# Opening a transformer block with a pair of column blocks: the convolution's first gate and value product made together, in a fixed order

## The chip, the cores and the metric

The kernel runs on one core of one Trainium2 chip. The metric is the device time of the whole program in microseconds, the median over several runs. TensorE (PE) does matrix products, VectorE (DVE) and ScalarE (ACT) elementwise work, GpSimd (POOL) very little here; SyncE (SP) issues nearly all DMAs. Each engine takes its instructions in one order that is fixed when the program is built; semaphores make an instruction wait for another engine or a DMA.

## The reference

One block on 256 positions of width 4096, batch 1, all in float32. Only the beginning matters for this case:

```
xn   = rms_norm(x, norm_in_g)
proj = xn @ w_in                       # 4096 x 14336 columns
q, k, v, z_a, a_c, g_c, z_c = split(proj, 7 parts of 2048 columns)
y_a  = rms_norm(chunked_attention(q, k, v), ...) * silu(z_a)      # 16 heads of 128
u    = a_c * sigmoid(g_c)              # then a causal depthwise convolution of 31 taps
u    = silu(layer_norm(conv(u) + b_dw)); y_c = rms_norm(u @ w_pw + b_pw, ...) * silu(z_c)
h    = x + concat(y_a, y_c) @ w_out
h    = h + sigmoid(rms_norm(h) @ w_ple_gate + b) * (p @ w_ple);  out = rms_norm(h, final_g)
```

## The kernel before

**Three products for one.** Every float32 operand is split into a high part in the matmul's format `fp32r` and the remainder, also in `fp32r`: for weights `wh` (ScalarE, `parts_of`, L197) and `wl` (VectorE, L198), for activations the two halves of a `big_t` tile. A product of a 128-row block of weights with 128 positions is three matmuls of 512 columns: high by high, low by high, high by low.

**Operands from x.** `x` comes in eight pieces of 512 columns (`xin`). Each piece is turned by eight transposes of 128x128 (L156, four to a PSUM tile `tmp_ps`) and split: ScalarE writes the high half with the norm's weight (L142), VectorE the low half (L143). The two blocks of one PSUM tile go one after the other: the second block's L142 waits for the first block's L143. Each piece gives four of the 32 row blocks (k-blocks) in the list `xT`. The division by the root mean square, `r_x`, comes at the end of each product, so sums of squares (L485, ScalarE, two per piece) are all that is needed of x's norm.

**Seven products for eight.** `mixed_product` makes two column blocks of 512 at a time, for two halves of 128 positions, over 16 pairs of k-blocks. A plain pair takes 8 products (24 matmuls, L361). A pair with a star in the order list takes seven (21 matmuls) by sums of weights (`ua`, `ub`, L414 to L419, VectorE, each split as well) and sums of activations (`xS`, `combine_again`: one addition L278, four of 128x128 L260 to L263, one split L266 and L267). The seven-product pairs also write four helper banks of PSUM. Weight tiles `wt` have 5 buffers, `wh` and `wl` 3 each.

**The opening.** `gate_0 = product(...)` makes the first gate block alone: one column block, 32 k-blocks by 6 matmuls (L211). Meanwhile `load_x` brings the eight pieces of `x`, and `combine_again` makes `xS` of the first four. Its first two k-blocks use weights loaded at once by ScalarE's DMA queue (`w_first`), the order of these first steps is fixed (`pin`), the rest is left to the scheduler. Ahead of all that, five matmuls on zeros (`WARM`, L114) keep TensorE at work. Then `glu_conv(0)` makes the first value block `acca`, again 192 matmuls by `product` (L211), and multiplies it with the gate's sigmoid.

**What follows.** For each of four groups: `glu_conv(c)` (a pair of column blocks of a and g), then `heads(g)`: q and k as one pair of column blocks, v by `product`. The convolution's 31 taps by 4 blocks are 124 VectorE instructions per group (L586, L590); they wait in a list `later`, and each step of a product moves a few of them into the program (`fill`): 4 per pair of k-blocks in the paired products and 2 per step in v. The scheduler then decides where in VectorE's queue they stand. The order of pairs in these stages is

```
early = units("1 3 5 7 0* 9 2* 11 4* 13 6* 15 8 10 12 14")
```

Of the kernel before, what the change touches and what calls it, by code (L numbers as in the profile page):

```python
# [16 lines left out]
P = 128  # L17
NB = 512
KC = 2
FIRST = 2  # L20
WARM = 5
# [5 lines left out]
def hybrid_block(  # L27
# [70 lines left out]
    w_first = []  # L98
    for k in range(FIRST):
        t = wpool.tile([P, KC, NB], F32, tag="w", name="wt")  # L100
        nc.scalar.dma_start(t[:, 0, :], w_in0[k * P : (k + 1) * P, o_g : o_g + NB])
        w_first.append(t)
# [10 lines left out]
    for _ in range(WARM):  # L113
        pin(nc.tensor.matmul(idle_ps, idle[:, :P], idle, start=True, stop=True))  # L114
# [15 lines left out]
    nc.tensor.transpose(gin_ps[:, :KD], gin_rows, ident[:KD, :KD])  # L130
# [34 lines left out]
    def transposed_split(src, dst, g, col0, **kw):  # L165

        for pair in range(2):
            blocks = (2 * pair, 2 * pair + 1)
            for b, pt in zip(blocks, transposed(src, blocks, **kw)):
                split_from_psum(dst, b, pt, g[:, col0 + b : col0 + b + 1])  # L170

# [32 lines left out]
    def accumulate(acc, h, lhs, kb, wh, wl, k, kblocks, kinds=range(3), then=lambda ins: None):  # L204
# [3 lines left out]
        for kind in kinds:  # L208
            a, b = ((xh, wh), (xl, wh), (xh, wl))[kind]
            then(  # L210
                nc.tensor.matmul(  # L211
                    acc, a, b[:, k, :],
                    start=kb == 0 and kind == 0, stop=kb == kblocks - 1 and kind == 2,
                )
            )

    def product(w, col, lhs, kblocks, pool=None, tag="acc", ahead=None, given=(), fills=2):
# [4 lines left out]
        starts = list(range(len(given))) + list(range(len(given), kblocks, KC))  # L222
        for k0 in starts:
            kc = 1 if k0 < len(given) else min(KC, kblocks - k0)
            if k0 < len(given):
                wh, wl = given[k0]
                for kind in range(3):
                    for h in range(NH):
                        accumulate(acc[h], h, lhs, k0, wh, wl, 0, kblocks, (kind,))
                continue  # L230
            wh, wl = weight_parts(w, col, k0, kc)
            for k in range(kc):
                for h in range(NH):
                    accumulate(acc[h], h, lhs, k0 + k, wh, wl, k, kblocks)
                if ahead and given and k0 + k == len(given):
                    ahead(k0)
            if ahead:
                ahead(k0 + kc)
            fill(fills)
# [14 lines left out]
    def combined_parts(dst, at, s, a, a01, a11, g):  # L254
# [5 lines left out]
        nc.vector.tensor_tensor(s3, a00, a10, ALU.subtract)  # L260
        stt(s5, a11, g, a10, ALU.mult, ALU.subtract)
        stt(s2, s5, -1.0, a00, ALU.mult, ALU.subtract)
        stt(s4, a01, g, s2, ALU.mult, ALU.add)  # L263
        hi, lo = dst[:, at : at + 2, 0, :], dst[:, at : at + 2, 1, :]
        src = s.rearrange("q (i t) -> q i t", t=T)
        nc.scalar.copy(hi, src)  # L266
        nc.vector.tensor_tensor(lo, src, hi.bitcast(F32), ALU.subtract)  # L267

    def combine(dst, at, pts, g):
# [3 lines left out]
        combined_parts(dst, at, s, a[:, :T], pts[1][:, :P], pts[1][:, P:], g[:, 1:2])  # L273

    def combine_again(dst, at, t, i, rows):

        a, s = rows
        nc.vector.tensor_tensor(  # L278
            a.rearrange("q (i t) -> q i t", t=T), t[:, i : i + 2, 0, :].bitcast(F32),
            t[:, i : i + 2, 1, :].bitcast(F32), ALU.add,  # L280
        )
        combined_parts(dst, at, s, a[:, :T], a[:, T : T + P], a[:, T + P :], 1.0)
# [34 lines left out]
    early = units("1 3 5 7 0* 9 2* 11 4* 13 6* 15 8 10 12 14")  # L317
# [3 lines left out]
    def mixed_product(  # L321
        w, col, lhs, comb, order, on_helpers, ahead=None, fills=0, on_begin=None, apart=NB,
        left=(),
    ):

# [31 lines left out]
        def add(name, x, w2, n, final):  # L357

            for kind, (a, b) in enumerate(((x[0], w2[0]), (x[1], w2[0]), (x[0], w2[1]))):
# [6 lines left out]
                begun.add(name)  # L366

# [3 lines left out]

        last_seven = max(n for n, (_, seven) in enumerate(order) if seven)
        for n, (pair, seven) in enumerate(order):
            if ahead:
                ahead(pair)
            wts = []
            for k in range(2):
                wt = wpool.tile([P, 2, NB], F32, tag="w", name="wt")
                kb = 2 * pair + k
                rows = w[kb * P : (kb + 1) * P, :]  # L380
                nc.sync.dma_start(
                    wt,
                    bass.AP(
                        tensor=rows.tensor, offset=rows.offset + col,
                        ap=[list(rows.ap[0]), [apart, 2], [1, NB]],
                    ),
                )
                wts.append(wt)
            if n >= len(order) - n_left:
# [3 lines left out]
                fill(fills)  # L393
                continue
            if not seven:
                for k in range(2):
                    wh, wl = parts_of(wts[k], 2)[0]
                    for j in range(2):
                        for h in range(NH):
                            name = (("P2", "P3"), ("P4", "X"))[h][j]  # L400
                            add(name, block(2 * pair + k, h), (wh[:, j], wl[:, j]), n, k == 1)
                fill(fills)
# [42 lines left out]
            fill(fills)  # L445
# [19 lines left out]
    def scaled_pair(w, col, apart, order, r, fills):  # L465

        t, z = sum_tiles()

        def on_helpers(helper):
            nc.scalar.activation(z[0][0], helper["P1"], AF.Identity, scale=r[:, :1])  # L470
# [4 lines left out]
        c = mixed_product(w, col, xT, xS, order, on_helpers, fills=fills, apart=apart)  # L475
# [21 lines left out]
    squares = [[partial(square_sum, ssq_x[:, h, :1], x_first[:, h, :]) for h in range(NH)]]  # L497

    def load_x(c):
        xin = act.tile([P, NH, NB], F32, tag="act", name="xin")  # L500
        loaded = nc.sync.dma_start(
            xin, x[0, :, c * NB : (c + 1) * NB].rearrange("(h q) n -> q h n", q=P)
        )
        xT.append(big_tile())
        if c == 1:
            pin(loaded)
            transposed_split(xin, xT[-1], g_in, 4 * c, then=pin)
        else:
            transposed_split(xin, xT[-1], g_in, 4 * c)
        squares.append(  # L510
            [partial(square_sum, ssq_x[:, h, c : c + 1], xin[:, h, :]) for h in range(NH)]
        )
        while len(squares) > (0 if c == D // NB - 1 else 2):
            later.extend(squares.pop(0))

    def first_operands():

        given = []
        xT.append(big_tile())
        for blocks in ((0,), (1,), (2, 3)):  # L520
            for b, pt in zip(blocks, transposed(x_first, blocks)):
                made = split_from_psum(xT[0], b, pt, g_in[:, b : b + 1])
                for ins in made:
                    pin(ins)
            if len(given) < FIRST:
                parts, made = parts_of(w_first[len(given)], 1)
                for ins in made:
                    pin(ins)
                given.append(parts)
        return given, made  # L530

# [19 lines left out]
    def load_ahead(kb):  # L551

        if kb == KD // 2:
            load_parameters()
        if kb % 4 == 2 and kb // 4 + 1 < D // NB:
            load_x(kb // 4 + 1)

    given, made = first_operands()
    with tc.issue_after(made[0].ins), tc.issue_after(made[1].ins):
        gate_0 = product(w_in0, o_g, xT, KD, ahead=load_ahead, given=given)  # L560
    fill(len(later))
    r_x = rstd_of(ssq_x, D, "r_x")

    prm_ps = tmp_psum()
    nc.tensor.transpose(prm_ps[:, :n_rows], prm_rows, ident[:n_rows, :n_rows])
    prm = cpool.tile([P, n_rows], F32, name="prm")
    nc.vector.tensor_copy(prm, prm_ps[:, :n_rows])
# [3 lines left out]
    dps = tmp_psum()  # L571
    for j in range(DWC):
        nc.tensor.transpose(
            dps[:, j * DWR : (j + 1) * DWR], dw_rows[:, j, :], ident[:DWR, :DWR]
        )
    nc.vector.tensor_copy(
        dw.rearrange("q (b j) t -> q j t b", j=DWC),
        dps[:, : DWC * DWR].rearrange("q (j t b) -> q j t b", j=DWC, t=TAPS),
    )
# [15 lines left out]
    def glu_conv(c):  # L595
        if c == 0:
            sg = spool.tile([P, NH, NB], F32, tag="stage", name="sg")
            for h in range(NH):
# [544 lines left out]
```

## Time and profile before

| | |
|---|---|
| median of 3 runs | 2048.15 us (2047.39 to 2050.24) |
| the profiled execution's own time | 2047.85 us |
| its span, first to last instruction | 2046.1 us |
| TensorE busy | 2026.5 us (99%), 9131 matmuls |
| VectorE busy | 1852.8 us (91%) |
| ScalarE busy | 1167.5 us (57%) |
| first gate block, x loaded | 0 to 59.8 us |
| first value block | 59.8 to 103.9 us |
| glu_conv(1), heads(0): q and k, v | 103.9 to 190.2, to 277, to 320 us |

The profiled execution is 0.3 us under the median, and 1.75 us of it lie outside the span. In a row of the timeline stand start, duration, engine, line, operation, output and inputs, shape and count, and in brackets the idle time before it with what ended that. A row of a group has count, busy time and mean duration in ns, then the idle time just ahead. [...]

### The profile page before, as it was taken

What the parts mean: (1) busy time and instruction counts of PE and PEld (TensorE: products, weight loads), DVE (VectorE), ACT (ScalarE), POOL (GpSimd) and SP (SyncE); (2) the same over time, 40 slices, a digit from 0 to 9 for tenths busy, and PEclk for the clock granted to TensorE, in tenths of its full rate; (3) what the DMA queues carried; (4) which work ended last, traced back from release to release, by engine and by line L of the source; (5) the groups of instructions that cost most, each with busy time, mean ns of one, the idle gap of its engine ahead of it and who ended that gap; (6) DMA issues with size and microseconds to landing.
All of it is one profiled execution on the core that took longest, in us unless ns stands there. A gap on an engine that the chain in (4) does not pass through costs nothing.

```text
span 2046.1 us, 25964 instructions
## 1 busy us (share of the span) xinstructions
PE 2026.5 (99%) x9131; PEld 1667.0 (81%) x9131; DVE 1852.8 (91%) x2629; ACT 1167.5 (57%) x1503; POOL 9.8 (0%) x19
## 2 busy tenths in 40 slices
PE   9999999999999999999999999999999999999997
PEld 7888888887888788888888888888888888888876
DVE  7599999899887998865889999999999999999998
ACT  7445535554455536575556656676565666655555
POOL 0000000000000000000000000000000000000000
PEclk9999999999999999999999999999999999999999
DMA  8666665665656656555666566676656656566765
GB/s 284 186 193 208 190 193 174 196 196 190 186 188 196 198 185 189 180 186 197 193 209 200 194 216 200 217 236 206 214 199 208 210 188 207 202 220 205 236 207 179
DMA packets 166236, 412.28 MB, mean 201 GB/s; under 512 B 13006, under 2 KB 16222, under 8 KB 166106
## 3 DMA queue, kind: packets, MB, share of 16 engines
q1 hardware_dynamic: 165818, 410.11, 61.5%
q8 instruction: 71, 1.16, 0.2%
q10 hardware_dynamic: 288, 0.52, 0.1%
q14 instruction: 59, 0.48, 0.1%
HBM read 406.39 MB, written 4.19 MB: 201 GB/s over the span
## 4 chain that ended last, share of the span: by engine, by line
PE 89%; DVE 8%; issue 2%; DMA 1%; ACT 1%; SPq 0%; POOLq 0%; POOL 0%; ACTq 0%; DVEq 0%
PE acc L361 54%; PE acc L211 18%; PE acc_P L361 14%; DVE wl L198 3%; DVE cv L590 2%; PE tmp_ps L156 1%; DMA wt<-in_w_in_dram 1%; DVE ul L198 1%; PE tmp_ps L754 0%; PE tmp_ps L772 0%; DVE z L477 0%; PE tmp_ps L739 0%; ACT wh L197 0%; PE acc L350 0%; DVE ub L418 0%
## 5 line engine op out<-in xcount | busy, mean ns | idle before, releaser
L197 ACT CAST wh<-wt 128x1024 fp32r<-128x1024 f32 (+1 forms) x740 | 722.7, 985 | 616.8 <-PE acc L361 337.7
L361 PE MATMUL acc<-wh,big_t 128*128 128x512 f32 x3438 | 1064.0, 391 | 0.1
L198 DVE TENSOR_TENSOR wl<-wt,wh 128x1024 fp32r<-128x1024 f32 (+1 forms) x740 | 835.2, 1139 | 113.3 <-ACT wh L197 108.6
L361 PEld LDWEIGHTS acc<-wh,big_t 128*128 128x128 f32 x3438 | 643.7, 188 | 132.9 <-DVE z L869 0.6
L361 PE MATMUL acc<-wl,big_t 128*128 128x512 f32 x1719 | 664.5, 391 | 1.1 <-DVE wl L198 1.1
L361 PEld LDWEIGHTS acc<-wl,big_t 128*128 128x128 f32 x1719 | 322.1, 188 | 71.1 <-DVE wl L198 4.3
L211 PE MATMUL acc<-wh,big_t 128*128 128x512 f32 x1072 | 334.6, 393 | 1.0 <-DVE big_t L143 0.8
L211 PEld LDWEIGHTS acc<-wh,big_t 128*128 128x128 f32 x1072 | 201.1, 189 | 42.5 <-DVE big_t L143 1.1
L211 PE MATMUL acc<-wl,big_t 128*128 128x512 f32 x536 | 209.0, 391 | 0.0
L590 DVE SCALAR_TENSOR_TENSOR cv<-uT,dw,cv 128x237 f32<-128x237 f32 (+26 forms) x480 | 203.8, 467 | 0.9
L197 ACT CAST uh<-ub 128x1024 fp32r<-128x1024 f32 x112 | 117.8, 1052 | 116.2 <-DVE ub L419 101.7
L361 PE MATMUL acc_P<-uh,big_t 128*128 128x512 f32 x570 | 174.5, 391 | 0.0
L197 ACT CAST uh<-ua 128x1024 fp32r<-128x1024 f32 x112 | 118.0, 1054 | 58.6 <-DVE ua L415 52.3
L198 DVE TENSOR_TENSOR ul<-ub,uh 128x1024 fp32r<-128x1024 f32 x112 | 136.8, 1222 | 9.1 <-ACT uh L197 8.0
L198 DVE TENSOR_TENSOR ul<-ua,uh 128x1024 fp32r<-128x1024 f32 x112 | 136.7, 1221 | 0.5
L361 PEld LDWEIGHTS acc_P<-uh,big_t 128*128 128x128 f32 x570 | 105.9, 188 | 24.6 <-ACT uh L197 3.4
L211 PEld LDWEIGHTS acc<-wl,big_t 128*128 128x128 f32 x536 | 101.0, 188 | 20.9
L361 PE MATMUL acc_P<-ul,big_t 128*128 128x512 f32 x285 | 109.4, 392 | 1.5 <-DVE ul L198 1.5
L414 DVE TENSOR_TENSOR ua<-wt 128x512 f32<-128x512 f32 x112 | 77.0, 688 | 21.7 <-DMA wt<-in_w_in_dram 17.5
L415 DVE TENSOR_TENSOR ua<-wt 128x512 f32<-128x512 f32 x112 | 76.9, 686 | 3.1 <-DMA wt<-in_w_in_dram 3.1
L419 DVE TENSOR_TENSOR ub<-ub,wt 128x512 f32<-128x512 f32 x112 | 77.0, 688 | 1.0
L418 DVE TENSOR_TENSOR ub<-ua,wt 128x512 f32<-128x512 f32 x112 | 76.9, 687 | 0.2
(215 smaller groups left out, 1368.1 us busy)
## 6 DMA issues: line engine op xcount, KB each, us to landing
wt<-in_w_in_dram SPq DMA_DIRECT2D x447, 512.0 KB, 3.8
wt<-in_w_out_dram SPq DMA_DIRECT2D x128, 512.0 KB, 4.3
wt<-in_w_ple_gate_dram SPq DMA_DIRECT2D x128, 512.0 KB, 4.0
wt<-in_w_pw_dram SPq DMA_DIRECT2D x32, 512.0 KB, 3.9
hc<-in_x_dram SPq DMA_DIRECT2D x8, 512.0 KB, 5.5
wt<-in_w_ple_dram SPq DMA_DIRECT2D x8, 512.0 KB, 4.4
xin<-in_x_dram SPq DMA_DIRECT2D x7, 512.0 KB, 8.2
out_dram<-hc SPq DMA_DIRECT2D x12, 256.0 KB, 2.7
```

The lines of the kernel that those rows point to most:

```text
L156: nc.tensor.transpose(pt[:, i * T + h * P : i * T + (h + 1) * P], src[:, h, b * P : (b + 1) * P], ident,)
L197: nc.scalar.copy(wh[:, :kc, :], wt[:, :kc, :]),
L198: nc.vector.tensor_tensor(wl[:, :kc, :], wt[:, :kc, :], wh[:, :kc, :].bitcast(F32), ALU.subtract),
L211: nc.tensor.matmul(acc, a, b[:, k, :], start=kb == 0 and kind == 0, stop=kb == kblocks - 1 and kind == 2,)
L361: nc.tensor.matmul(banks[name], a, b, start=name not in begun, stop=final and ends[name] == n and kind == 2 and not (left and name in "P2 ...
L414: plus(ua[:, 0], w0[:, 0], w0[:, 1])
L415: plus(ua[:, 1], w0[:, 1], w1[:, 1])
L418: plus(ub[:, 0], ua[:, 0], w1[:, 1])
L419: plus(ub[:, 1], ub[:, 0], w1[:, 0])
L590: nc.vector.scalar_tensor_tensor(cv[:, i, PAD - k :], uT[:, i, : T + k - PAD], dw[:, b, k : k + 1], cv[:, i, PAD - k :], ALU.mult, ALU.add,)
```

## The change

The first gate block and the first value block become one `mixed_product` with the order list `first`: 16 pairs, of which 8, 10 and 12 take seven products. Its first nine pairs are written out by hand in `first_pairs`, every instruction pinned. Pair n needs k-blocks 2n and 2n+1, while piece n of x is loaded, transposed and split, so x is complete after eight pairs. `xS` is made of the last four pieces (`xT[4]` to `xT[7]`), between pairs 5 and 8, and `early` becomes a list whose seven-product pairs are 8, 10, 12 and 14. The parameters' transposes and copies (`parameters`, L565 to L576 before) move into this stage. `WARM` is (5, 3, 2): five matmuls on zeros as before, three behind the transpose of the norm's weights, two behind the first transposes of x. The high parts of the first two k-blocks' weights are made by VectorE (`high`). The fills are 0 in the first stage, 3 and 4 in turn in glu_conv(1) to (3), 3 in q and k, and 4 in v. Cut to its core:

```diff
-FIRST = 2
-WARM = 5
+WARM = (5, 3, 2)
...
+    w_first = [wpool.tile([P, 2, NB], F32, tag="w", name="wt") for _ in range(2)]
+    for j, col in enumerate((o_a, o_g)):
+        nc.scalar.dma_start(w_first[0][:, j], w_in0[:P, col : col + NB])
+    nc.scalar.dma_start(w_first[1], two_columns(w_in0, 1, o_a, o_g - o_a))
...
+    warm(WARM[0])
...
+    pin(nc.tensor.transpose(gin_ps[:, :KD], gin_rows, ident[:KD, :KD]))
+    warm(WARM[1])
...
-    early = units("1 3 5 7 0* 9 2* 11 4* 13 6* 15 8 10 12 14")
+    first = units("0 1 2 3 4 5 6 7 9 8* 11 10* 13 12* 15 14")
+    early = units("9 11 13 15 8* 1 10* 3 12* 5 14* 7 0 2 4 6")
...
+    def first_pairs(add):
+        def load(n): ...          # weights of pair first[n], and piece n of x
+        def parts(n, k): ...      # wh (ScalarE), wl (VectorE) of k-block k of pair n
+        def high(k, cols=slice(0, 2)):
+            pin(nc.vector.tensor_copy(made[0, k][0][:, cols], w_first[k][:, cols]))
+        def low(k): ...           # wl of the first pair
+        def operands(c, *blocks): # transposes of one PSUM tile, then L142/L143 block by block
+            pts = transposed(xin[c], blocks, then=pin)
+            for b, pt in zip(blocks, pts):
+                both = split_from_psum(xT[c], b, pt, g_in[:, 4 * c + b : 4 * c + b + 1])
+                last[:] = [*(pin(i) for i in both), *last_transpose]
+        def products(n, k, *kinds): ...
+        load(1)
+        for k in range(2):
+            made[0, k] = part_tiles()
+        for j in range(2):
+            high(0, slice(j, j + 1))
+        operands(0, 0)
+        low(0)
+        warm(WARM[2])
+        products(0, 0, (0,))
+        high(1)
+        operands(0, 1)
+        low(1)
+        products(0, 0, (1,), (2,))
+        operands(0, 2, 3)
+        for k in range(2):
+            parts(1, k)
+        products(0, 1, (0,), (1,), (2,))
+        for n in range(1, n_x + 1):
+            split = None
+            if n < n_x:
+                load(n + 1)
+                parts(n + 1, 0)
+            if n == 4:
+                load_parameters()
+            for h in range(NH):
+                pin(square_sum(ssq_x[:, h, n - 1 : n], xin[n - 1][:, h, :]))
+            if n > n_x // 2:
+                c = n - 1
+                comb = spool.tile([P, 2, NB], F32, tag="stage", name="comb")
+                split = combine_again(
+                    xS[c // 2], 2 * (c % 2), xT[c], 0, (comb[:, 0], comb[:, 1]), pin
+                )
+            products(n, 0)
+            if n < n_x:
+                xT.append(big_tile())
+                for blocks in ((0, 1), (2, 3)):
+                    operands(n, *blocks)
+                parts(n + 1, 1)
+            if split:
+                split()
+            products(n, 1)
+        parameters()
+        nc.vector.tensor_reduce(r_x, ssq_x, AX.X, ALU.add)
+        rsqrt(r_x, r_x, D)
...
-            acca = product(w_in0, o_a, xT, KD)
+            sg, gate = scaled_pair(
+                w_in0, o_a, o_g - o_a, first, r_x, (0,), begin=first_pairs
+            )
...
-            sg, gate = scaled_pair(w_in0, o_a + c * NB, o_g - o_a, early, r_x, 4)
+            sg, gate = scaled_pair(w_in0, o_a + c * NB, o_g - o_a, early, r_x, (3, 4))
...
-        q, k = scaled_pair(w_in0, o_q + g * NB, o_k - o_q, early, r_x, 4)
+        q, k = scaled_pair(w_in0, o_q + g * NB, o_k - o_q, early, r_x, (3,))
...
-        accv = product(w_in0, o_v + g * NB, xT, KD)
+        accv = product(w_in0, o_v + g * NB, xT, KD, fills=4)
```

More of the change, by code (lines that the diff above doesn't have):

```diff
@@ L112, in hybrid_block, with warm @@
     idle_ps = tmp_psum()
-    for _ in range(WARM):
-        pin(nc.tensor.matmul(idle_ps, idle[:, :P], idle, start=True, stop=True))
+    def warm(n):
+        for _ in range(n):
+            pin(nc.tensor.matmul(idle_ps, idle[:, :P], idle, start=True, stop=True))
+    warm(WARM[0])
     ident = cpool.tile([P, P], F32, name="ident")
@@ L215, in accumulate, with product @@
             )
-    def product(w, col, lhs, kblocks, pool=None, tag="acc", ahead=None, given=(), fills=2):
+    def product(w, col, lhs, kblocks, pool=None, tag="acc", fills=2):
         acc = [
@@ L221, in product @@
         ]
[L222 to L230, printed above, removed]
+        for k0 in range(0, kblocks, KC):
+            kc = min(KC, kblocks - k0)
             wh, wl = weight_parts(w, col, k0, kc)
@@ L321, in mixed_product @@
     def mixed_product(
-        w, col, lhs, comb, order, on_helpers, ahead=None, fills=0, on_begin=None, apart=NB,
-        left=(),
+        w, col, lhs, comb, order, on_helpers, ahead=None, fills=(0,), on_begin=None, apart=NB,
+        left=(), begin=None,
     ):
@@ L370, in block, with add_plain @@
             return [t[:, kb % 4, q, h * P : (h + 1) * P] for q in range(2)]
+        def add_plain(n, k, wh, wl, **kw):
+            pair = order[n][0]
+            for j in range(2):
+                for h in range(NH):
+                    name = (("P2", "P3"), ("P4", "X"))[h][j]
+                    add(name, block(2 * pair + k, h), (wh[:, j], wl[:, j]), n, k == 1, **kw)
+        done, after = 0, ExitStack()
+        if begin:
+            done, behind = begin(add_plain)
+            for ins in behind:
+                after.enter_context(tc.issue_after(ins.ins))
         last_seven = max(n for n, (_, seven) in enumerate(order) if seven)
         for n, (pair, seven) in enumerate(order):
+            if n < done:
+                continue
             if ahead:
@@ L396, in mixed_product @@
                 for k in range(2):
[L397 to L402, printed above, removed]
+                    add_plain(n, k, *parts_of(wts[k], 2)[0])
+                fill(fills[n % len(fills)])
                 continue
@@ L516, in first_operands @@
[L516 to L530, printed above, removed]
+    xS = [None] * 2 + [big_tile(upool) for _ in range(2)]
@@ L549, in load_parameters, with parameters @@
             nc.sync.dma_start(dw_rows[lo:hi], taps[lo:hi])
[L551 to L565, printed above, removed]
     prm = cpool.tile([P, n_rows], F32, name="prm")
-    nc.vector.tensor_copy(prm, prm_ps[:, :n_rows])
     ln_g, ln_b, bdw, ga, gc, gp = (prm[:, a : a + n] for a, (_, n) in zip(at, rows))
     dw = spool.tile([P, KCW, TAPS], F32, name="dw", bufs=1)
[L571 to L574, printed above, removed]
-        )
[L576 to L579, printed above, removed]
+    def parameters():
+        prm_ps = tmp_psum()
+        nc.tensor.transpose(prm_ps[:, :n_rows], prm_rows, ident[:n_rows, :n_rows])
+        nc.vector.tensor_copy(prm, prm_ps[:, :n_rows])
+        dps = tmp_psum()
+        for j in range(DWC):
+            nc.tensor.transpose(
+                dps[:, j * DWR : (j + 1) * DWR], dw_rows[:, j, :], ident[:DWR, :DWR]
+            )
+        nc.vector.tensor_copy(
+            dw.rearrange("q (b j) t -> q j t b", j=DWC),
+            dps[:, : DWC * DWR].rearrange("q (j t b) -> q j t b", j=DWC, t=TAPS),
+        )
     conv = []
@@ L813, in hybrid_block @@
     assert n_g == CW // NB
-    xS = [big_tile(upool) for _ in range(2)]
-    for c in range(4):
-        rows = spool.tile([P, 2, NB], F32, tag="stage", name="comb")
-        combine_again(xS[c // 2], 2 * (c % 2), xT[c], 0, (rows[:, 0], rows[:, 1]))
     glu_conv(0)
@@ L864, in on_helpers @@
             helper_sums(helper, z)
-        acc = mixed_product(w_in0, col + c0 * NB, xT, xS, order, on_helpers, ahead=ahead, fills=2)
+        acc = mixed_product(w_in0, col + c0 * NB, xT, xS, order, on_helpers, ahead=ahead, fills=(2,))
         for h, j in QUARTERS:
@@ L973, in gated_pair @@
         acc = mixed_product(
[L974 removed]
+            w_ple_gate[0], c0 * NB, hT, hS, order, on_helpers, ahead=ahead, fills=(4,),
             on_begin=on_begin,
```

153 lines of the change are left out of this document (77 added, 76 removed).

## The prediction

> **What bounds the kernel now.** I read the page's busy shares first, then the waits of TensorE by stretch, then the timeline of the first 25 us.
>
> ```profile
> PE 2026.5 (99%) x9131; PEld 1667.0 (81%) x9131; DVE 1852.8 (91%) x2629; ACT 1167.5 (57%) x1503; POOL 9.8 (0%) x19
> ```
> ```profile
> 22.34:59.80 37.46, 37.46 (x186) 31.31 (x185) 31.82 (x60) 29.05 (x59) 0.71 (x1) 1.00 0.73 241
> 59.80:103.90 44.10, 44.10 (x198) 36.57 (x197) 21.34 (x19) 18.92 (x19) 0.00 (x0) 1.00 0.63 191
> 103.90:190.20 86.30, 85.85 (x382) 70.43 (x381) 85.88 (x139) 43.42 (x48) 0.00 (x0) 1.00 0.63 195
> 190.20:277.00 86.80, 86.47 (x391) 71.42 (x389) 86.24 (x137) 45.42 (x50) 0.30 (x1) 1.00 0.63 201
> ```
>
> The columns of the second fence are the stretch, its length, then busy time of PE, PEld, DVE, ACT and POOL, clock, DMA share and GB/s. TensorE is the bound everywhere: the stage that makes the first value block (59.8 to 103.9 us) has it busy throughout with VectorE at half load, the paired stages behind it have both full. So time can only come from fewer matmuls, or from gaps between them, and can be lost wherever VectorE is late. The price of a matmul:
>
> ```profile
> 22.34 0.39 PE L211 MATMUL acc<-wl,big_t 128*128 128x512 f32 x1
> 22.57 0.61 PE L211 MATMUL acc<-wh,big_t 128*128 128x512 f32 x2
> 23.02 0.39 PE L211 MATMUL acc<-wl,big_t 128*128 128x512 f32 x1
> ```
>
> From 22.34 to 23.02 three have started: 0.68 / 3 = 0.227 us each. The gaps that TensorE has in the stages that the change touches:
>
> ```profile
> PE acc L361 <- DVE wl L198: 1.1, 2, 0.6
> PE tmp_ps L739 <- DVE z L477: 0.9, 3, 0.3
> PE acc_P L361 <- DVE ul L198: 0.6, 2, 0.5
> ```
>
> These are its waits between 103.9 and 730 us (total, times, longest), all for VectorE: 2.6 us to win there. The opening has more:
>
> ```profile
> 1.18 2.31 PE L114 MATMUL tmp_ps<-idle 128*128 128x512 bf16 x5 [1.18 <-DVE ssq_f L951]
> 3.42 0.31 PE L130 MATMUL tmp_ps<-ident,gin_rows 32*128 32x32 f32 x1
> 4.62 2.48 PE L156 MATMUL tmp_ps<-ident,xin 128*128 128x128 f32 x8 [0.88 <-DMA xin<-in_x_dram]
> 6.75 2.05 PE L211 MATMUL acc<-wh,big_t 128*128 128x512 f32 x4
> 9.45 0.82 PE L211 MATMUL acc<-wh,big_t 128*128 128x512 f32 x2
> 11.02 1.07 PE L211 MATMUL acc<-wh,big_t 128*128 128x512 f32 x4
> 15.00 0.50 PE L211 MATMUL acc<-wh,big_t 128*128 128x512 f32 x1 [0.20 <-ACT big_t L142]
> 16.29 0.50 PE L211 MATMUL acc<-wh,big_t 128*128 128x512 f32 x1 [0.79 <-DVE big_t L143]
> ```
>
> Four matmuls take 2.05 us at 6.75 and 1.07 at 11.02: until about 9.9 us TensorE runs at half speed (0.43 us a matmul), although the clock column reads 1.00. Full speed comes 5.3 us after its last long pause (0.88 us, ending at 4.62).
>
> **Fewer matmuls.** Before, 2 x 192 matmuls; after, 16 x 24 - 3 x 3 = 375. Nine less: 9 x 0.227 = **-2.0 us**, on the path everywhere. The five more on zeros lie in pauses.
>
> **The start.** Now TensorE works nearly without pause from 1.18: five on zeros, the transpose at 3.42, three on zeros to about 5.0, two transposes of x, two on zeros, first product at about 6.4 (6.75 before). If full speed again needs 5.3 us of work without a long pause, it comes at 6.5 instead of 9.9. Walking the fixed order with the durations below, pair 0 then runs from 6.4 to 12.5; pair 1 waits 0.4 us for `wh` and 0.75 us for `wl`, since ScalarE and VectorE do x's blocks 2 and 3 first; its last matmul, the 48th with 16 transposes behind it, starts at 19.8. Before, that count is reached at 22.34, but with 24 transposes, eight more at 0.87 us in all, so at 21.5 like for like: **-1.65 us**. If full speed comes at 9.9 all the same, the walk gives -0.45; without pair 1's waits -2.8. I take -1.65, as nothing but the pause distinguishes the two starts.
>
> [...]
>
> **The fixed order of pairs 1 to 8.** This is the largest term. Two blocks of one PSUM tile follow in lockstep:
>
> ```profile
> 7.13 0.47 ACT L142 ACTIVATE big_t<-tmp_ps,g_in 128x256 fp32r<-128x256 f32 x1
> 7.96 0.48 DVE L143 SCALAR_TENSOR_TENSOR big_t<-tmp_ps,g_in,big_t 128x256 fp32r<-128x256 f32 x1
> 8.47 0.48 ACT L142 ACTIVATE big_t<-tmp_ps,g_in 128x256 fp32r<-128x256 f32 x1 [0.87 <-DVE big_t L143]
> 8.98 0.49 DVE L143 SCALAR_TENSOR_TENSOR big_t<-tmp_ps,g_in,big_t 128x256 fp32r<-128x256 f32 x1 [0.54 <-ACT big_t L142]
> ```
>
> The second L143 starts 1.02 us after the first, 0.54 of it idle. The scheduler of before put two tiles side by side (or `wl` between); the hand order does tile by tile, so VectorE waits 0.54 us twice a piece. The other durations of this stretch:
>
> ```profile
> L198 DVE TENSOR_TENSOR wl<-wt,wh 128x1024 fp32r<-128x1024 f32 x29 | 35.5, 1225 | 26.6 <-ACT wh L197 26.2 <-PE tmp_ps L156 0.4
> L143 DVE SCALAR_TENSOR_TENSOR big_t<-tmp_ps,g_in,big_t 128x256 fp32r<-128x256 f32 x24 | 10.6, 479 | 0.3 <-ACT big_t L142 0.3
> L278 DVE TENSOR_TENSOR comb<-big_t 128x512 f32<-128x512 f32 x4 | 2.7, 687 | 0.1
> L267 DVE TENSOR_TENSOR big_t<-comb,big_t 128x512 fp32r<-128x512 f32 x4 | 2.7, 686 | 0.7 <-ACT big_t L266 0.7
> L576 DVE COPY dw<-tmp_ps 128x496 f32<-128x496 f32 x1 | 1.1, 1085 | 0.2 <-PE tmp_ps L573 0.2
> L567 DVE COPY prm<-tmp_ps 128x112 f32<-128x112 f32 x1 | 0.3, 274 | 0.7 <-PE tmp_ps L565 0.7
> L197 ACT CAST wh<-wt 128x1024 fp32r<-128x1024 f32 x29 | 30.5, 1051 | 28.9 <-PE acc L211 27.9 <-issue 1.0
> ```
> ```profile
> 149.26 2.35 DVE L198 TENSOR_TENSOR wl<-wt,wh 128x1024 fp32r<-128x1024 f32 x2
> 24.89 0.29 DVE L260 TENSOR_TENSOR comb<-comb 128x128 f32<-128x128 f32 x1
> 25.74 0.29 DVE L263 SCALAR_TENSOR_TENSOR comb<-comb 128x128 f32<-128x128 f32 x1
> ```
>
> Two `wl` in a row take 2.35, so one costs 1.13 where it needn't wait; the four small operations take 25.74 + 0.29 - 24.89 = 1.14. TensorE needs 24 x 0.227 + 0.87 = 6.3 us a pair with its eight transposes. VectorE's round, from the first L143 of one piece to that of the next, by the built program's order: to the fourth L143 2.5; then the next pair's second `wl`, which waits for a `wh` that ScalarE starts only behind the fourth L142, so it starts at 3.45 (0.5 idle) and ends at 4.6; the split of the sums 0.6; the following `wl` 1.13; the addition 0.7 and four small ones 1.14: **8.15 us**. Pairs 1 to 4 have no sums: 5.8, hidden. Pair 5 has no split yet: 7.5. Pair 7 holds the parameters' copies too, 0.27 + 1.09 less overlap: 9.4. Over TensorE's 6.3 that is 1.2, 1.85 and 3.1 us late, and pair 8 comes 0.87 sooner, having no transposes, with 0.6 of `ua` ahead of its `wl`. Against that stand 1.75 us in hand at pair 4 (`wl` is ready 5.9 us after piece 4's transposes start, wanted at 7.6) and the parameters' transposes, TensorE work that fills some 0.5. Walked step by step: 0.7 us of waits at pair 7's second block, 4.1 at pair 8's: **+4.8**. VectorE enters the seven-product pairs late, with the last sums still to make: two waits, for `ul` 0.35 and for `uh` of `ub` 1.2: **+1.55**. Then it has two plain pairs' slack and catches up. Bounds: waits shrink to 2.8 in all if the lockstep's 0.54 falls away, and grow to 9.6 if nothing overlaps (1.23 for each `wl`, and so on). I take 6.35, since every duration has its row.
>
> **The end of the stage.** The first sigmoid's table load moves:
>
> ```profile
> L599 ACT ACT_TABLE_LOAD x1 | 1.3, 1283 | 1.2 <-PE acc L211 1.2
> 190.99 1.15 ACT L606 ACTIVATE z<-z 128x512 f32<-128x512 f32 x2
> 193.02 0.38 PE L614 MATMUL tmp_ps<-ident,z 128*128 128x128 f32 x2
> ```
>
> Before, it sat under the value block's matmuls. Now it stands between pair 15's end and the sigmoids, as at 190.99 but 1.28 later, and the transposes (193.02 there, without a wait to speak of) stand 13 matmuls into the next stage: **+0.7** (0 to 1.3).
>
> **The taps.** The fills change, but the scheduler places taps by its own view. VectorE's built order has, from the end of the first stage on, 69, 69, 110, 69, 55, 69, 55 taps up to the end of each paired product, against 75, 69, 104, 69, 55, 73, 51. Ten taps of about 0.4 us move from full stages to v stages. q and k of the first groups get the pattern that waited before. **-0.8** (-2.5 to +1.7) of the 2.6 us of waits.
>
> **DMA.** Both openings need 1 MB of weights and 0.5 MB of x per 24 matmuls; at 241 GB/s (22.34 to 59.80) before. Nothing changes on the path; SP passes the six parameter rows earlier, in the DMA-bound first 12 us, hence the walk's late pair 1.
>
> **Sum.** 2047.85 - 2.0 - 1.65 + 4.8 + 1.55 + 0.7 - 0.8 = 2050.4 for a profiled run; with the 0.3 us between it and the median, **2050.7**. That is +2.5 us, within the 0.2% (4.1 us) that I take as the least a measurement tells.
>
> **Rivals.** *Faster: VectorE keeps up.* If its round is near 6.5 us, waits fall to 1: 2.0 + 1.65 + 0.8 - 1 - 0.7 = 2.75 less, 2045.4, and with the better start (2.8) 2044.2. For it: VectorE's busy part of a round is only about 6.7 us, and 22.34 to 59.80 shows it 85% busy with the same work and TensorE unhurt. Against: there the sums were spread over the whole stretch and the tiles interleaved; here every wait is built into the order. 27%.
>
> *Slower: VectorE is the bound of pairs 5 to 8 and the seven-product pairs.* One mechanism, with its durations unoverlapped: rounds of 8.0, 8.7 and 10.0, waits of 9.6: 2050.7 + 3.25 = 2054.0. It decides once the waits pass 8 us. For it: semaphore times between the engines, which my walk takes at 0.03 us. 20%.
>
> *The start isn't sooner*, full speed coming at 9.9 all the same: 2051.9; inside the forecast.
>
> **Numbers.** Forecast 53%: of it 42 land within 0.2% and 11 above. Rival one: 17 below, 10 within. Rival two: 19 above, 1 within. So faster 0.17, same 0.53, slower 0.30. Range: waits of 2.8 with the best start give 2043 to 2045; waits of 9.6 with the taps' bound 2056; an eighth cut off each side: 2044.0 to 2055.5.
>
> **What would show it.** Right: 375 matmuls in the stage; full speed near 6.5 us; DVE rounds of 8 us with waits of TensorE for `wl` around the eighth and ninth pair; a table load just behind the stage. Wrong: no wait of TensorE for VectorE before the seven-product pairs (rival one), or waits in every pair from the fifth on and through the stage (rival two), or waits after it that fall by more than 1 us.

## The result: slower by 0.25%, and the profile after

The changed kernel takes 2053.44 us (median of 11 runs, 2051.23 to 2056.09) against 2048.05 us beside it on the same chip: a ratio of 1.0025, 95% interval 1.0015 to 1.0034, or 5.4 us more. That lies in the predicted range, 2.7 us above the predicted 2050.7. The profiled execution took 2054.11 us, its span is 2052.3 against 2046.1.

The numbers of lines have moved: L142, L143, L197, L198 of the kernel before are now L155, L156, L203, L204; the paired matmuls are L367, the transposes of `z` L798. First the page's busy shares, then the stretches of the first stage and of the two behind it (stretch, length, then PE, PEld, DVE, ACT and POOL busy, clock, DMA share, GB/s):

```profile
PE 2028.0 (99%) x9127; PEld 1665.7 (81%) x9127; DVE 1871.7 (91%) x2657; ACT 1172.2 (57%) x1511; POOL 11.6 (1%) x19
```
```profile
0.00:21.34 21.34, 18.94 (x74) 12.12 (x75) 10.90 (x18) 9.30 (x17) 0.88 (x8) 1.00 0.78 250
21.34:60.84 39.50, 39.27 (x199) 32.54 (x197) 28.83 (x46) 29.40 (x60) 0.00 (x0) 1.00 0.76 252
60.84:77.27 16.43, 13.21 (x49) 9.81 (x47) 14.20 (x30) 10.50 (x17) 2.55 (x1) 0.90 0.37 113
77.27:108.33 31.06, 31.06 (x136) 25.49 (x137) 27.92 (x32) 17.47 (x21) 0.00 (x0) 1.00 0.74 236
108.33:195.58 87.25, 86.22 (x382) 70.22 (x380) 85.71 (x136) 45.60 (x51) 0.00 (x0) 1.00 0.61 193
```

One stretch of 16.4 us, pair 8 and its neighbours (pairs are counted by their place in the order, from 0), has TensorE idle for 3.2 us and its clock below 1. The timeline there, first VectorE's splits and copy, then ScalarE, then TensorE, and last a stretch by itself:

```profile
48.41 0.48 DVE L156 SCALAR_TENSOR_TENSOR big_t<-tmp_ps,g_in,big_t 128x256 fp32r<-128x256 f32 x1 [0.54 <-ACT big_t L155]
56.45 0.48 DVE L156 SCALAR_TENSOR_TENSOR big_t<-tmp_ps,g_in,big_t 128x256 fp32r<-128x256 f32 x1 [0.54 <-ACT big_t L155]
61.45 1.03 DVE L638 COPY dw<-tmp_ps 128x496 f32<-128x496 f32 x1
65.28 0.48 DVE L156 SCALAR_TENSOR_TENSOR big_t<-tmp_ps,g_in,big_t 128x256 fp32r<-128x256 f32 x1 [0.54 <-ACT big_t L155]
```
```profile
63.35 0.84 ACT L155 ACTIVATE big_t<-tmp_ps,g_in 128x256 fp32r<-128x256 f32 x2 [2.80 <-DVE big_t L156]
65.14 1.03 ACT L203 CAST wh<-wt 128x1024 fp32r<-128x1024 f32 x1
```
```profile
66.23 0.73 PE L367 MATMUL acc<-wh,big_t 128*128 128x512 f32 x2 [2.29 <-ACT wh L203]
67.55 0.50 PE L367 MATMUL acc<-wl,big_t 128*128 128x512 f32 x1 [0.59 <-DVE wl L204]
68.71 1.05 PE L367 MATMUL acc<-wh,big_t 128*128 128x512 f32 x2
69.99 1.05 PE L367 MATMUL acc<-wh,big_t 128*128 128x512 f32 x2
```
```profile
68.35:71.99 3.64, 3.64 (x10) 2.84 (x9) 3.64 (x10) 1.95 (x4) 1.98 (x1) 0.53 0.59 160
```

Start from TensorE: it waits 2.29 us for `wh`; ScalarE could begin that cast only at 65.14, since it waited 2.80 us for VectorE's split; VectorE was still at the last round's sums and at the parameters' copy (L638). The fourth split of a piece stands at 48.41, 56.45 and 65.28, so two rounds take 8.0 and 8.8 us; the walk (the prediction's count, step by step, of the fixed order) had 8.15 and 9.4. The waits are where the walk put them: by the distances of the matmuls' starts beyond 0.227 us (from 61.06 to 61.74 three start, 0.227 us apart, though a single one is 0.39 us long in the rows), 0.8 us in pair 7 and 3.4 in pair 8 (0.7 and 4.1 predicted). What the walk had not is the last fence: TensorE runs at half speed from 68.35 to about 71.7 (each matmul starts 0.43 us after the one ahead of it instead of 0.227), with the clock at 0.53. By the starts that costs another 1.6 us.

The opening of the changed kernel:

```profile
6.12 1.58 PE L367 MATMUL acc<-wh,big_t 128*128 128x512 f32 x4
8.12 0.44 PE L169 MATMUL tmp_ps<-ident,xin 128*128 128x128 f32 x2 [0.42 <-DMA xin<-in_x_dram]
8.32 1.18 PE L367 MATMUL acc<-wh,big_t 128*128 128x512 f32 x4
14.27 0.73 PE L367 MATMUL acc<-wh,big_t 128*128 128x512 f32 x2 [0.27 <-ACT wh L203]
15.53 0.50 PE L367 MATMUL acc<-wl,big_t 128*128 128x512 f32 x1 [0.53 <-DVE wl L204]
```

The first product starts at 6.12, the four at 8.32 run at full speed (1.18 us, where four at half speed took 2.05 in the kernel before), pair 1 waits as foreseen (0.43 and 0.70 us between starts beyond a matmul's own). A wait for `x` at 8.12 was not foreseen: the prediction saw nothing new on the path in the DMAs. The 48th matmul starts at 21.34, not at 19.8.

Behind the first stage, first its end, then TensorE's waits for VectorE from 104 to 730 us (total, times, longest):

```profile
109.38 1.28 ACT L665 ACT_TABLE_LOAD   x1
112.08 0.44 PE L673 MATMUL tmp_ps<-ident,z 128*128 128x128 f32 x2 [0.65 <-DVE z L666]
```
```profile
PE tmp_ps L798 <- DVE z L489: 2.6, 4, 1.2
PE acc_P L367 <- DVE ul L204: 0.8, 2, 0.5
PE tmp_ps L673 <- DVE z L666: 0.6, 1, 0.6
```

The waits for `wl` (1.1 before) are gone, those of the transposes for `z` have grown from 0.9 to 2.6. And the last value product has a wait that the trace of before had not:

```profile
877.64 5.02 ACT L756 ACTIVATE cv<-cv,prm 128x256 f32<-128x256 f32 x10
882.56 1.03 ACT L203 CAST wh<-wt 128x1024 fp32r<-128x1024 f32 x1
883.64 1.18 PE L217 MATMUL acc<-wh,big_t 128*128 128x512 f32 x4 [0.86 <-ACT wh L203]
```

Ten activations of the convolution's output stand ahead of a weight's cast on ScalarE; the waits around it add up to 1.9 us, and that product takes 46.1 us instead of 44.1.

### The profile page after: what moved, and what is told of

Same layout as the page of the kernel before. It is cut to its first block, busy times and chain, and to the rows that moved or that the text cites. A ratio compares the mean times of both kernels' runs of the same rounds, so it can differ in the third digit from the quotient of the medians.

```text
span 2052.3 us, 25989 instructions
## 1 busy us (share of the span) xinstructions
PE 2028.0 (99%) x9127; PEld 1665.7 (81%) x9127; DVE 1871.7 (91%) x2657; ACT 1172.2 (57%) x1511; POOL 11.6 (1%) x19
## 3 DMA queue, kind: packets, MB, share of 16 engines
q10 hardware_dynamic: 560, 1.05, 0.2%
## 4 chain that ended last, share of the span: by engine, by line
PE 88%; DVE 7%; issue 2%; ACT 1%; DMA 1%; ACTq 0%; POOLq 0%; POOL 0%; DVEq 0%; SPq 0%
PE acc L367 58%; PE acc_P L367 14%; PE acc L217 14%; DVE wl L204 2%; DVE cv L652 1%; DVE ul L204 1%; DMA wt<-in_w_in_dram 1%; PE tmp_ps L169 1%; ACT wh L203 1%; DMA xin<-in_x_dram 0%; DVE big_t L156 0%; PE tmp_ps L813 0%; PE tmp_ps L831 0%; DVE z L489 0%; PE tmp_ps L798 0%
## 5 line engine op out<-in xcount | busy, mean ns | idle before, releaser
L367 PE MATMUL acc<-wh,big_t 128*128 128x512 f32 x3658 | 1133.1, 392 | 3.1 <-ACT wh L203 2.8
L203 ACT CAST wh<-wt 128x1024 fp32r<-128x1024 f32 (+1 forms) x737 | 718.2, 984 | 589.6 <-PE acc L367 328.8
L204 DVE TENSOR_TENSOR wl<-wt,wh 128x1024 fp32r<-128x1024 f32 (+1 forms) x737 | 828.6, 1135 | 90.6 <-ACT wh L203 85.8
L367 PEld LDWEIGHTS acc<-wh,big_t 128*128 128x128 f32 x3658 | 685.0, 188 | 145.4 <-ACT wh L203 3.9
L367 PE MATMUL acc<-wl,big_t 128*128 128x512 f32 x1829 | 706.1, 391 | 1.3 <-DVE wl L204 1.3
L367 PEld LDWEIGHTS acc<-wl,big_t 128*128 128x128 f32 x1829 | 343.1, 188 | 75.2 <-DVE wl L204 3.9
L652 DVE SCALAR_TENSOR_TENSOR cv<-uT,dw,cv 128x250 f32<-128x250 f32 (+25 forms) x480 | 202.0, 462 | 1.2
L203 ACT CAST uh<-ub 128x1024 fp32r<-128x1024 f32 x115 | 121.0, 1052 | 124.4 <-DVE ub L428 106.9
L367 PE MATMUL acc_P<-uh,big_t 128*128 128x512 f32 x588 | 180.1, 391 | 0.4 <-ACT uh L203 0.3
L203 ACT CAST uh<-ua 128x1024 fp32r<-128x1024 f32 x115 | 121.1, 1053 | 60.1 <-DVE ua L424 55.7
L204 DVE TENSOR_TENSOR ul<-ub,uh 128x1024 fp32r<-128x1024 f32 x115 | 140.2, 1219 | 7.9 <-ACT uh L203 6.8
L204 DVE TENSOR_TENSOR ul<-ua,uh 128x1024 fp32r<-128x1024 f32 x115 | 140.0, 1218 | 1.5 <-ACT uh L203 1.1
L367 PEld LDWEIGHTS acc_P<-uh,big_t 128*128 128x128 f32 x588 | 109.2, 188 | 25.9 <-ACT uh L203 4.1
L367 PE MATMUL acc_P<-ul,big_t 128*128 128x512 f32 x294 | 113.0, 392 | 1.1 <-DVE ul L204 1.1
```

The costliest lines, as they stand in the source:

```text
L203: nc.scalar.copy(wh[:, :kc, :], wt[:, :kc, :]),
L204: nc.vector.tensor_tensor(wl[:, :kc, :], wt[:, :kc, :], wh[:, :kc, :].bitcast(F32), ALU.subtract),
L367: nc.tensor.matmul(banks[name], a, b, start=name not in begun, stop=final and ends[name] == n and kind == 2 and not (left and name in "P2 ...
L652: nc.vector.scalar_tensor_tensor(cv[:, i, PAD - k :], uT[:, i, : T + k - PAD], dw[:, b, k : k + 1], cv[:, i, PAD - k :], ALU.mult, ALU.add,)
```

## The experiments

Every kernel is the changed one with the edit shown, timed beside the kernel before on one chip for each group of runs. "Ratio" is to the kernel before, with its 95% interval; the changed kernel's is 1.0025 (1.0015 to 1.0034).

**Splits interleaved over two PSUM tiles.**

```diff
-                for blocks in ((0, 1), (2, 3)):
-                    operands(n, *blocks)
+                pts = {}
+                for blocks in ((0, 1), (2, 3)):
+                    pts.update(zip(blocks, transposed(xin[n], blocks, then=pin)))
+                for b in (0, 2, 1, 3):
+                    ...                      # L155 and L156 of block b
```

> In pairs 1 to 7 both tiles' transposes of x come first and the four splits then go in block order 0, 2, 1, 3, so that neighbouring splits read different PSUM tiles; the rest is the changed kernel. Theory A (the order makes VectorE late: it waits 0.54 us for ScalarE twice a piece, its round is some 8 us against TensorE's 6.3, and the 2.45 us pause in pair 8 brings the half-speed stretch after it): VectorE's round falls to about 7.1 us, TensorE's waits at the second blocks of pairs 7 and 8 fall from 4.1 us to 1 or less, no pause is over 2 us and the half-speed stretch of 1.5 us behind it goes; the program is 3 to 5 us faster than the changed kernel. Rival B (the amount of VectorE's work in these pairs, not its order): the waits stay within 1 us of 4.1, and the time within 1 us.

2049.75 us, ratio 1.0002 (0.9993 to 1.0010): the loss is gone, some 4.7 us. VectorE's splits as a group from 12 to 78 us, in the changed kernel and then in this one; then this kernel's rounds and stretches:

```profile
L156 DVE SCALAR_TENSOR_TENSOR big_t<-tmp_ps,g_in,big_t 128x256 fp32r<-128x256 f32 x30 | 13.8, 481 | 10.5 <-ACT big_t L155 10.5
```
```profile
L156 DVE SCALAR_TENSOR_TENSOR big_t<-tmp_ps,g_in,big_t 128x256 fp32r<-128x256 f32 x30 | 13.5, 481 | 5.6 <-ACT big_t L155 4.7
```
```profile
51.99 0.88 DVE L156 SCALAR_TENSOR_TENSOR big_t<-tmp_ps,g_in,big_t 128x256 fp32r<-128x256 f32 x2
59.00 0.88 DVE L156 SCALAR_TENSOR_TENSOR big_t<-tmp_ps,g_in,big_t 128x256 fp32r<-128x256 f32 x2
```
```profile
20.74:58.74 38.00, 38.00 (x194) 31.99 (x192) 29.92 (x51) 29.74 (x61) 0.00 (x0) 1.00 0.81 275
58.74:70.77 12.03, 11.91 (x54) 9.22 (x53) 11.88 (x23) 8.87 (x15) 1.74 (x1) 1.00 0.37 118
```

The same 30 splits wait 4.7 us for ScalarE instead of 10.5, the round is 7.0 us, and TensorE is busy without a pause in pairs 2 to 7. The clock is 1.00 behind them, so the half speed is gone too, and its 1.6 us are part of the 4.7. The first stage ends at 102.2 us instead of 108.3. In this profiled execution, which is 2.45 us above the median, 3.4 us of that are lost again later (0.7 in the next q and k, 1.2 in the v product behind them, the rest mostly behind the last value product), so the size is the medians' 4.7. Theory A holds as written. One thing besides the order differs: the scheduler put the parameters' copies behind pair 8 here; the run on them, below, prices that.

**The sigmoid's table at the start.**

```diff
-    pin(nc.scalar.activation(idle_out, idle[:, :1], AF.Identity))
+    pin(nc.scalar.activation(idle_out, idle[:, :1], AF.Sigmoid))
```

> The activation at the very start asks for the sigmoid's table, so that no table load is left behind the first stage. If that load is on the path: the waits at the stage's end (0.81 and 0.18 us, for the first sigmoids) go, and the time is 0.7 to 1.0 us less than the changed kernel's. Rival: the sigmoids are late for another reason (VectorE's sums): waits and time stay within 0.3 us.

2054.05 us, ratio 1.0019 (1.0010 to 1.0028). In the trace the stage behind the first takes 86.3 us instead of 87.25 (86.12 before, between the same two first matmuls), and the transposes have no wait worth a bracket:

```profile
110.97 0.38 PE L673 MATMUL tmp_ps<-ident,z 128*128 128x128 f32 x2
```

So the load is worth 0.95 us by the trace; the medians' difference of 1.2 us agrees but is inside the intervals. Two rows of this run matter for the half speed, the stretches 65 to 67 and 67 to 71.6 us:

```profile
65.00:67.00 2.00, 1.76 (x3) 1.00 (x4) 2.00 (x4) 2.00 (x6) 0.00 (x0) 0.50 0.00 0
67.00:71.60 4.60, 4.60 (x12) 3.58 (x11) 3.90 (x11) 2.20 (x4) 2.55 (x1) 0.50 0.63 158
```

The program up to there differs only in the table, and half speed lasts some 6.5 us instead of 3.35.

**Taps in the numbers of before.** `(3, 4)` and `(3,)` become `(4,)`, and `fills=4` becomes 2.

> The numbers of taps behind each pair or piece are those of before (4 in paired products, 2 in single ones); all else is the changed kernel. If the new spread costs time, the waits of TensorE ahead of the q and k transposes (2.3 us at 504, 1.7 us at 281) go back to those of before (1.2 and 0.8), the 1.9 us around 884 in the last value product goes, and the time is 2 to 3 us less. Rival: those waits come from where the scheduler happens to put taps and not from the numbers: they move, and the time stays within 1 us.

2053.74 us, ratio 1.0021 (1.0013 to 1.0030). The last value product is back at 44.1 us, the waits of the transposes for `z` fall from 2.6 to 0.5:

```profile
PE acc L367 <- DVE wl L204: 1.1, 2, 0.6
PE acc_P L367 <- DVE ul L204: 0.8, 1, 0.8
PE tmp_ps L673 <- DVE z L666: 0.6, 1, 0.6
PE tmp_ps L798 <- DVE z L489: 0.5, 2, 0.3
```

From the end of the second stage to the last matmul this kernel is 1.0 us shorter than the kernel before, the changed kernel 0.75 longer: the spread costs 1.75 us in the traces. The medians, 0.8 us apart in ratio, can't show that; the runs with all three edits and without the taps' edit, below, can.

**Without the five zeros behind the first transposes.** `WARM = (5, 0, 0)`.

> The three and two matmuls on zeros behind the first transposes are left out; all else is the changed kernel. If they bring full speed sooner by closing the pauses: full speed comes at about 9.9 us as in the kernel before instead of 7.3 to 8, and the 48th matmul starts 0.5 to 1.7 us later, of which the waits for pair 1's weights may hide up to 1.1. Rival: the moment of full speed doesn't hang on the pauses, and it stays near 7.5 us, with the time within 0.3 us.

2057.54 us (5 runs), ratio 1.0033 (1.0020 to 1.0045). The matmuls of pair 0:

```profile
8.41 2.06 PE L367 MATMUL acc<-wh,big_t 128*128 128x512 f32 x4
10.26 1.91 PE L367 MATMUL acc<-wl,big_t 128*128 128x512 f32 x4
12.48 2.07 PE L367 MATMUL acc<-wh,big_t 128*128 128x512 f32 x8
```

Four in 2.06 us at 8.41, eight in 2.07 at 12.48: full speed comes at about 12.0 instead of 7, later still than the 9.9 that was expected. The 48th matmul starts at 22.31; in the profiled executions of the ten kernels that have the zeros it lies between 19.80 and 21.34. So closing the pauses is worth 1.0 to 2.5 us at that point, by one execution without the zeros; in the whole time the difference is inside the intervals. The walk's premise, that the pauses put off full speed, holds; its 5.3 us of work do not come as a fixed time: seven of those ten make their first products, at 5.80 to 6.17 us, at full speed already (four in 1.20 us at 5.89 in the run with the taps of before), and three don't.

**Zeros in the pause of pair 8.**

```diff
+            if n == n_x:
+                zero_ps = tmp_psum()
+                for _ in range(8):
+                    pin(nc.tensor.matmul(zero_ps, idle[:, :P], idle, start=True, stop=True))
             products(n, 1)
```

> Eight matmuls on zeros (0.21 us each) stand ahead of the second block of pair 8, where TensorE paused for 2.45 us; all else is the changed kernel. If the pause is what brings half speed: the stretch of matmuls at 0.43 us behind it (1.6 us lost in the changed kernel's trace, 2.2 to 3.3 us in those of the other kernels with this pause) goes, the wait itself stays, and the time is 1 to 2 us less than the changed kernel's. Rival: half speed there has another cause (a moment of its own, or load): it stays, and the time is within 0.5 us.

2053.13 us, ratio 1.0015 (1.0006 to 1.0024), 2 us under the changed kernel's ratio, though the two intervals overlap; the trace decides.

```profile
62.92 1.90 PE L602 MATMUL tmp_ps<-idle 128*128 128x512 bf16 x8
66.92 0.62 PE L367 MATMUL acc<-wh,big_t 128*128 128x512 f32 x2
71.46 0.74 PE L367 MATMUL acc<-wl,big_t 128*128 128x512 f32 x2 [0.82 <-DVE wl L204]
```

Work on zeros does nothing for the sums, yet the half-speed stretch is gone: two matmuls in 0.62 us behind it, where the changed kernel took 1.05. So the pause itself was the cause. From the 48th matmul to the stage's end this kernel is 1.0 us shorter, not 1.6, since waits for VectorE come in its place: 0.98 us for `wl` (by the starts; 0.82 in the row at 71.46) and 0.68 for `uh` at 75.5. Slow matmuls had given VectorE time to catch up. The scheduler also put the parameters' transposes and copies behind the zeros; the next run moves them alone and keeps the half speed, so it is the zeros that remove it. What the copies add to these two waits isn't separated.

**The parameters behind the stage's pairs.** The call `parameters()` moves from the end of `first_pairs` to behind `scaled_pair`.

> The parameters' transposes and copies move from pair 7 to behind the first stage's pairs; all else is the changed kernel. In the run with the splits interleaved over two tiles they had left pair 7 too, so this run prices them alone. If VectorE's lateness in pair 8 is their 1.36 us (0.27 and 1.09) and the lockstep makes the rest: the pause of 2.45 us falls to about 1.1 to 1.4 and the half-speed stretch may go, 1.3 to 3 us less in the first stage, with up to 1 us back at its end, where VectorE makes the copies ahead of the products. Rival: the copies are most of it: waits in pair 8 fall under 1 us.

2055.05 us, ratio 1.0024 (1.0015 to 1.0034): no gain.

```profile
64.76 0.73 PE L367 MATMUL acc<-wh,big_t 128*128 128x512 f32 x2 [1.49 <-ACT wh L203]
66.08 0.50 PE L367 MATMUL acc<-wl,big_t 128*128 128x512 f32 x1 [0.59 <-DVE wl L204]
68.82 1.05 PE L367 MATMUL acc<-wh,big_t 128*128 128x512 f32 x2
```

The pause shrinks by 0.8 us, somewhat less than expected, the half speed stays, and the copies cost 1.2 us at the stage's end (the next stage takes 88.5 us instead of 87.25). The copies are not what the interleaved run won by; the order of the splits is.

**All three, and all but the taps.** Interleaved splits, early table and taps of before; then the first two alone.

> Splits interleaved over two tiles in pairs 1 to 7, the sigmoid's table asked for at the start, and the taps in the numbers of before, together; all else is the changed kernel. If the three costs add: the profiled last matmul comes at 2035.3 - 2.7 (interleaved) - 1.0 (table) - 1.1 (taps) = 2030.5 us against 2029.1 in the kernel before, so within 0.1% of it; where the start goes as in the changed kernel's trace, without the pause of 1.4 us in pair 0, 2029. Rival: the waits that one of them frees come back in another place, and it stays at 2032 or above.

> Splits interleaved over two tiles and the sigmoid's table at the start, with the changed kernel's spread of taps. If the spread costs 1 us beside these two: 1 us slower than the kernel that also has the taps of before, with the wait of 1.1 us around 880 in the last value product in it; last matmul at about 2031.6. Rival: the spread helps where VectorE isn't late: as fast or faster.

All three: 2046.31 us, ratio 0.9982 (0.9973 to 0.9991). This beats both kernels, the kernel before by 3.8 us. Without the taps' edit: 2048.98 us, ratio 0.9996 (0.9987 to 1.0005). The last matmuls of 512 columns start at 2027.7 and 2029.4, 2.8 and 2.2 us sooner than expected; the expectation went out from the profiled execution of the interleaved kernel, which was 2.45 us above that kernel's median. The difference of 1.7 (2.7 in the medians) is the taps' spread, as in the run on it alone. The waits for `z` from 104 to 730 us say the same, with the taps of before and with the spread:

```profile
PE tmp_ps L805 <- DVE z L489: 0.5, 2, 0.3
```
```profile
PE tmp_ps L805 <- DVE z L489: 2.6, 4, 1.2
```

**Which number of the spread.** As all three, but three steps per piece of a value product; then as all three, but the paired products' numbers of the change (3 and 4, and 3).

> As the kernel with all three edits (interleaved splits, early table, taps of before), but three steps of the queue behind each piece of a value product instead of two. If the cost of the new spread sits in the value products, because the queue's steps there are ScalarE's as well (ten activations of 0.5 us in a row ahead of a weight's cast at 877.6 to 882.6 in the changed kernel, TensorE waiting 1.9 us): the last value product has a wait between those of two (0) and four (2.0 us), some 0.5 to 2, and the program is about as much slower. Rival: the cost lies in the paired products' counts: no wait there, and the time within 0.5 us.

> As the kernel with all three edits, but with the changed kernel's numbers of taps in the paired products (3 and 4 in turn, and 3); value products keep two. If the value products carry the cost: no wait around 880, the last value product at 44.1 us as in the kernel before, and the time within 1 us of the kernel with all three. If the paired products' counts carry some of it: waits ahead of the q and k transposes of the first two groups come back (1.5 and 2.0 us), and it is 1 to 3 us slower.

Three steps: 2048.98 us, ratio 0.9996 (0.9987 to 1.0006), some 3 us slower than two by the ratios and 2.3 us by the traces' last matmul of 512 columns. The last value product takes 44.75 us, 0.6 more than with two steps, as expected; but the q and k stage ahead of it, whose numbers are the same in both kernels, takes 97.2 instead of 94.3: most of the cost moved there, which was not expected. The other missed by far: 2094.36 us (4 runs), ratio 1.0217 (1.0203 to 1.0231). A gate stage, q and k, and a value product of the changed kernel move 16 x 3.5 + 16 x 3 + 16 x 4 = 168 steps of the queue, those of the kernel before 160, and those here 136. At the end of the last group the convolution's norm is still in the queue, and all of it is paid in the open:

```profile
PE tmp_ps L744 <- DVE sq L707: 12.2, 1, 12.2
PE acc L217 <- ACT big_t L773: 10.1, 1, 10.1
PE tmp_ps L838 <- ACT s L831: 6.8, 4, 2.4
```

These waits are 29 of the 48 us that it is slower than all three. The four steps in the value products are thus what the smaller numbers in the pairs need, and can't be judged without them.

## Why the prediction came out as it did

The time fell into the range and the waits into their places, but 2050.7 was 2.7 us low, and the forecast itself ("within 0.2%") just missed: 5.4 us is 0.25%, with an interval (0.15 to 0.34%) that takes 0.2% in. By number the result is nearest to the rival "VectorE is the bound" (2054.0); by mechanism it isn't that rival, whose waits were 9.6 us where 4.8 were measured. The terms, in the profiled execution:

| term | predicted | measured |
|---|---|---|
| nine matmuls fewer | -2.0 | -2.0 |
| start, at the 48th matmul | -1.65 | -0.2 |
| fixed order, waits in pairs 7 and 8 | +4.8 | +4.2 |
| waits in the seven-product pairs | +1.55 | +0.6 |
| half speed after the pause | not foreseen | +1.6 |
| table load | +0.7 | +0.95 |
| taps and all behind the second stage | -0.8 | +0.75 |
| rest of the first two stages | | +0.3 |
| sum, to the last matmul of 512 columns | +2.6 | +6.2 |

The waits came out 1.55 us lower than predicted and the half speed, which had no term, cost 1.6: that these two nearly cancel is in part luck, so the time is a better fit than the account behind it. (The sum misses by 3.6 us and the median by 2.7, mostly since the profiled execution lies 0.7 us above the median.)

**Fixed order: right.** The lockstep of two splits of one tile, 0.54 us each time, makes VectorE's round too long, and undoing it (7.0 us a round) wins the loss back. The waits were 0.6 us less than the walk's, the longest round being 8.8 us and not 9.4. Those of the seven-product pairs were 0.9 less. The half speed ahead of them, which the walk lacked, gave VectorE time: in the run with zeros, without half speed, they are 0.98 and 0.68, together 1.66 where 1.55 was predicted, though the first is for `wl` and not for `ul`, and the parameters' copies stand elsewhere in that run.

**What lay behind a wait: the step that failed.** The walk priced a pause of TensorE at its own length. The prediction looked at full speed only in the opening. Here the pause was followed by 3.35 us at half speed in the changed kernel (+1.6 us) and about twice that in the run with the early table, and zeros in the pause removed it. In the changed kernel 2.29 us and 0.59 us of idleness within 3.6 us were enough. What sets the length of the slow stretch no run shows.

**The start: right in mechanism, mis-sized.** Pair 0 ended at 13.8 instead of 12.5, by a wait for `x`'s second block (0.42 us in the row at 8.12) and by full speed at about 7 instead of 6.5; pair 1's waits came as walked. The ten executions with the zeros put the 48th matmul at 19.80 to 21.34; the walk's 19.8 was the best of them, the changed kernel's profiled one the worst. The wait for `x` varies among them: the fifth product starts 0.37 to 2.04 us after the fourth, and in the run with interleaved splits the row is

```profile
8.44 0.44 PE L169 MATMUL tmp_ps<-ident,xin 128*128 128x128 f32 x2 [1.26 <-DMA xin<-in_x_dram]
```

The term should have been a range from -0.2 to -1.7.

**The table: right**, 0.95 us where 0.7 was predicted.

**The taps: wrong sign.** The prediction counted taps in VectorE's order. It did not look at what else waits in the same queue: the ten activations on ScalarE ahead of a weight's cast in the last value product cost 2.0 us. The waits for `z` behind q and k grew by 1.7 us; the numbers of the spread bring them, as three runs show, but which taps stand there to cause them was not traced.

## What to carry to other kernels

When an order is written out by hand, walk every engine that takes part in it, and put work on two buffers side by side where two engines hand one buffer back and forth; here that was 4.7 us, half speed included. Price a pause of TensorE with the slow stretch that may follow it, or fill it: 1.49 and 0.59 us close together were enough here. Give the opening a range and not one number: ten traces of it differed by 1.5 us. A queue that feeds work into other stages has a sum that must be spent and steps of several engines: change one of its numbers and look at the last stage first.

## What the runs showed of the hardware

Half speed after a pause: 2.29 us of waiting for `wh` and 0.59 for `wl`, then a clock of 0.53 from 68.35 to 71.99 us. In the run with the parameters moved, 1.49 and 0.59 us were enough too (a clock of 0.57 from 66 to 70 us), while 1.26 us in the opening of the run with interleaved splits (the row at 8.44 above) were not: the next four products ran at full speed (1.18 us at 8.64). In the opening of the kernel before, the clock column read 1.00 while matmuls took 0.43 us apiece, so there only the distance of the starts tells. And the same opening reaches full speed at different times: the first four products take 1.58 us in the changed kernel (6.12) and 1.20 us in the run with the taps of before:

```profile
5.89 1.20 PE L367 MATMUL acc<-wh,big_t 128*128 128x512 f32 x4
```
